# A hybrid decoder layer on one core: the ends of two feed-forwards, one place in the mixer and the start are put in another order

## The chip, the cores and the metric

The kernel runs on one core of one Trainium2 chip. A core has five engines that run beside each other, each with its own instruction stream: TensorE (PE) multiplies matrices into PSUM, VectorE (DVE) and ScalarE (ACT) work on elements, GpSimd (POOL) does small things here, and SyncE (SP) issues most transfers. The metric is the device time of one execution in microseconds (us).

## The reference, cut to what matters

One decoder layer over 512 tokens of width 1024:

```
h = x + 1/2 * SwiGLU_1(RMSNorm(x))                # 1024 -> 2816 -> 1024
z = RMSNorm(h) @ W_in                             # q, k, v | gla q, k, v, gate rank, out gate
A = sliding_window_attention(q, k, v, sinks)      # 8 heads of 64, window 128
B = RMSNorm(gated_linear_attention(...)) * silu(gate)
h = h + concat(A, B) @ W_out
h = h + 1/2 * SwiGLU_2(RMSNorm(h))
h = h + sigmoid(RMSNorm(h) @ W_g) * RMSNorm(p @ W_p)
```

All of it is in float32.

## The kernel before, in words

The 512 tokens are four tiles of 128 (`h[0]` to `h[3]`). Every large product is three matmuls (`mm3`): both operands are split into a high part in fp32r and the rest, also fp32r, and hi·hi, hi·lo and lo·hi are added in PSUM. Weights come as "units" of 1 MB or 512 KB (`W`): a transfer that SP issues into `wraw`, a cast on ScalarE to `whi`, a subtraction on VectorE to `wlo` (`split`, L140 and L141; in the first two units every second subtraction is GpSimd's). `W.get` splits the unit that is asked for and some ahead; a third number says how far ahead.

A norm of one tile has five steps: two squares with a running sum on ScalarE (`norm_squares`), the mean on VectorE and the power on GpSimd (`norm_factor`), the scaling on VectorE (`norm_scaled`), eight 128x128 transposes on TensorE into two PSUM banks and, for each bank, a cast `nhi` on ScalarE and a subtraction `nlo` on VectorE (`norm_transpose`). The gain of a norm lies in SBUF spread over 128 partitions; `gain_tile` gets it by a broadcasting transfer of 512 KB.

The stages follow each other: feed-forward 1 (`pg`, `pu`, `pd`), the mixer (`pe`, an embedding product; `kvr`, `aq`, `gqk`, `gv`, `gog`, the input projections; attention and the gated linear attention), the output projection `wo`, feed-forward 2, and the gate `pgt`. A scheduler writes the engines' streams in the order of the code, except where `on_pe` and `in_order` tie a step behind the last instruction of TensorE, or of TensorE, ScalarE and VectorE. So these lists of steps are the order: `last_tiles` for the end of a feed-forward (last down products of a tile, the update of `h`, its norm), and the long list that ends with `gla_mix` for the mixer. An engine's stream runs in order: what waits holds what is behind it.

Four places matter here.

- The start. SP asks for the first tile of x, the spread gain of the first norm, the second tile, the first two weight units and the other two tiles. The first product covers tiles 0 and 1 (columns 0 to 256), once with the gate's weights and once with the up weights.
- The end of feed-forward 1. `pe` of tiles 0 and 1 stands on TensorE behind the transposes of tiles 0 and 1 (`ntr_mx`), and its bank is one that the last update of `h[3]` has to read out first.
- The mixer. `turn_decay` transposes decayed keys in three pieces `kdt0` to `kdt2`, one after the other, into a pool of two banks (`psG`), and ScalarE copies each to `kdT`. Later four `gla_out` steps give `o0` to `o3`, and `gla_mix` their transposes `otr`.
- The end of feed-forward 2. The units of the gate's weights (`wraw135` and on) are split between the norms; `split_gates` asks for the first. Then `pgt` runs over two halves of the columns and four tiles; the last one is done in two parts of 256 columns.

Of the kernel before, what the change touches and what calls it, by code (L numbers as in the profile page):

```python
# [152 lines left out]
def hymba_kernel(tc, A, out):  # L153
# [457 lines left out]
    for t in range(0, NT, 2):  # L611
        eo = mp.tile([P, 8, 256], F32, name=f"eo{t}", tag="e", bufs=2).rearrange("p (t a) c -> p t (a c)", t=2)
        for i in range(2):
# [5 lines left out]
            if t + i in (1, 2):  # L619
                turned[0](t + i + 1)  # L620
# [377 lines left out]
    with tc.tile_pool(name="ffn2p", bufs=1, reuse_waits="tile") as fp:  # L998
# [39 lines left out]
        def split_gates():  # L1038
            W.get(("pg", 0, 0), 0)
# [88 lines left out]
```

## Time and profile before

| | us |
|---|---|
| median of 3 runs | 1008.62 (1008.01 to 1010.85) |
| the profiled execution | 1008.22 |
| span of its instructions | 1006.5 |
| TensorE busy | 971.2 |
| VectorE busy | 645.0 |
| ScalarE busy | 394.5 |

The profile is of one execution. Its span runs from the first to the last instruction, and 1.7 us lie around it. TensorE is busy for 96% of the span; what it waited for is listed by line in a view of its own. The profile also gives for each stretch the clock that was granted to TensorE, as a share of the full one (1.00 is 2.4 GHz, 0.50 is 1.2 GHz). Busy TensorE at 0.50 counts as busy.

### The profile page before, as it was taken

How to read it: one execution, taken by the hardware profiler on the slowest of the kernel's cores; microseconds unless marked ns; L12 is line 12 of the kernel's file. 1: busy time of each engine (PE TensorE's matmuls, PEld its weight loads, DVE VectorE, ACT ScalarE, POOL GpSimd, SP SyncE). 2: the span in 40 equal slices, each digit the busy share in tenths (PEclk: the TensorE clock that was granted, in tenths of full speed). 3: DMA queues.
4: the chain of work that ended last, by engine and by line, in shares of the span. 5: the costliest groups of instructions: out<-in, count | busy, mean ns of one | idle time of the engine just before them, and what ended most of it. 6: DMA issues, size and time to landing. Idle time of an engine off the chain costs nothing.

```text
span 1006.5 us, 12373 instructions
## 1 busy us (share of the span) xinstructions
PE 971.2 (96%) x5090; PEld 807.4 (80%) x5090; DVE 645.0 (64%) x811; ACT 394.5 (39%) x569; POOL 43.7 (4%) x55
## 2 busy tenths in 40 slices
PE   5999999999999989998998999999999999999898
PEld 5988888888888879876766789888888888888687
DVE  6567667576675764775766364766677675757652
ACT  5443333333333245585455243333344333332441
POOL 4000000000000010200002010000000000000010
PEclk9999999999999999999998999999999999999999
DMA  8715133141330255220213246142252523303231
GB/s 290 250 47 168 41 126 125 46 167 40 126 105 1 88 186 184 88 85 1 58 50 98 84 163 242 42 168 84 96 205 75 169 83 106 124 1 104 74 126 53
DMA packets 74235, 109.91 MB, mean 109 GB/s; under 512 B 5937, under 2 KB 55234, under 8 KB 74178
## 3 DMA queue, kind: packets, MB, share of 16 engines
q1 hardware_dynamic: 72450, 102.82, 30.4%
q0 software_dynamic: 1728, 6.29, 1.8%
q8 instruction: 40, 0.66, 0.2%
q14 instruction: 17, 0.14, 0.0%
HBM read 100.72 MB, written 8.39 MB: 108 GB/s over the span
## 4 chain that ended last, share of the span: by engine, by line
PE 88%; DVE 6%; ACT 2%; DMA 2%; issue 1%; POOL 0%; SPq 0%; ACTq 0%; POOLq 0%; DVEq 0%
PE pg L199 24%; PE pu L199 24%; PE pd L199 20%; PE pgt L199 5%; PE wo L199 4%; PE aq L199 2%; PE pe L199 1%; PE kvr L199 1%; PE gqk L199 1%; PE gv L199 1%; PE gog L199 1%; DVE mx L724 1%; DMA wraw<-in_w_out_dram 1%; DVE wlo L141 1%; DVE e L722 1%
## 5 line engine op out<-in xcount | busy, mean ns | idle before, releaser
L140 ACT CAST whi<-wraw 128x1024 fp32r<-128x1024 f32 (+1 forms) x126 | 129.9, 1039 | 187.4 <-PE pd L199 136.3
L141 DVE TENSOR_TENSOR wlo<-wraw,whi 128x1024 fp32r<-128x1024 f32 (+1 forms) x124 | 149.9, 1215 | 56.0 <-ACT whi L140 53.7
L199 PE MATMUL pg<-nlo_f,whi 128*128 128x512 f32 (+1 forms) x384 | 143.0, 373 | 0.0
L199 PE MATMUL pg<-nhi_f,whi 128*128 128x512 f32 (+1 forms) x384 | 142.6, 373 | 0.2 <-ACT nhi_f L292 0.2
L199 PE MATMUL pu<-nhi_f,wlo 128*128 128x512 f32 (+1 forms) x384 | 142.6, 372 | 0.0
L199 PE MATMUL pg<-nhi_f,wlo 128*128 128x512 f32 (+1 forms) x384 | 142.6, 372 | 0.0
L199 PE MATMUL pu<-nlo_f,whi 128*128 128x512 f32 (+1 forms) x384 | 142.6, 372 | 0.0
L199 PE MATMUL pu<-nhi_f,whi 128*128 128x512 f32 (+1 forms) x384 | 142.4, 372 | 0.0
L199 PE MATMUL pd<-whi,ahi 128*128 128x512 f32 x312 | 121.4, 389 | 0.0
L199 PE MATMUL pd<-wlo,ahi 128*128 128x512 f32 x312 | 121.4, 389 | 0.0
L199 PE MATMUL pd<-whi,alo 128*128 128x512 f32 x312 | 120.6, 389 | 0.0
L391 DVE SCALAR_TENSOR_TENSOR h<-pd,h 128x512 f32<-128x512 f32 x116 | 76.5, 686 | 29.5 <-PE pd L199 29.5
L199 PEld LDWEIGHTS pg<-nhi_f,whi 128*128 128x128 f32 x384 | 72.3, 189 | 13.2 <-ACT nhi_f L292 0.7
L199 PEld LDWEIGHTS pg<-nlo_f,whi 128*128 128x128 f32 x384 | 72.6, 189 | 12.9 <-DVE nlo_f L293 0.6
L199 PEld LDWEIGHTS pg<-nhi_f,wlo 128*128 128x128 f32 x384 | 72.5, 189 | 12.5
L199 PEld LDWEIGHTS pu<-nhi_f,wlo 128*128 128x128 f32 x384 | 72.3, 188 | 12.5
L199 PEld LDWEIGHTS pu<-nhi_f,whi 128*128 128x128 f32 x384 | 72.2, 188 | 12.5
L199 PEld LDWEIGHTS pu<-nlo_f,whi 128*128 128x128 f32 x384 | 72.4, 188 | 12.3
L140 ACT CAST whi<-draw 128x1024 fp32r<-128x1024 f32 x35 | 36.8, 1053 | 96.9 <-PE pu L199 50.9
L431 DVE TENSOR_TENSOR cb<-pu,sg 128x512 f32<-128x512 f32 x44 | 30.3, 690 | 69.2 <-PE pu L199 69.2
L140 ACT CAST whi<-wpr 128x1024 fp32r<-128x1024 f32 x35 | 36.9, 1053 | 96.2 <-PE pu L199 58.2
L199 PEld LDWEIGHTS pd<-whi,ahi 128*128 128x128 f32 x312 | 58.6, 188 | 12.2
(243 smaller groups left out, 1466.5 us busy)
## 6 DMA issues: line engine op xcount, KB each, us to landing
wraw<-in_ffn_w_gate_dram SPq DMA_DIRECT2D x22, 1024.0 KB, 5.0
wraw<-in_ffn_w_up_dram SPq DMA_DIRECT2D x22, 1024.0 KB, 5.0
wpr<-in_ffn_w_down_dram SPq DMA_DIRECT2D x10, 1024.0 KB, 5.6
draw<-in_ffn_w_down_dram SPq DMA_DIRECT2D x10, 1024.0 KB, 5.2
wraw<-in_w_in_dram SPq DMA_DIRECT2D x8, 1024.0 KB, 4.9
wraw<-in_ple_w_gate_dram SPq DMA_DIRECT2D x4, 1024.0 KB, 4.8
h<-in_x_dram SPq DMA_DIRECT2D x4, 512.0 KB, 7.0
wraw<-in_ffn_w_down_dram SPq DMA_DIRECT2D x4, 512.0 KB, 3.4
```

The lines of the kernel that those rows point to most:

```text
L140: nc.scalar.copy(hi, v)
L141: (nc.gpsimd if u < 2 and i else nc.vector).tensor_tensor(lo, v, hi.bitcast(F32), op=ALU.subtract)
L199: last_pe[0] = nc.tensor.matmul(o, lhsT=l, rhs=r, start=start, stop=stop_, **kw).ins
L391: nc.vector.scalar_tensor_tensor(hs, x, 0.5, hs, ALU.mult, ALU.add)
L431: nc.vector.tensor_mul(cb[:, half].rearrange("p a c -> p (a c)"), pu, sg)
L722: nc.vector.tensor_add(half, sc[:, :, :, :nk], amask[:, 256 - nk:].unsqueeze(1).unsqueeze(1).broadcast_to([P, 2, 2, nk]))
L724: nc.vector.reduce_max(mxt.rearrange("p (g a) -> p g a", g=2)[:, :, 2 * a:2 * a + 2], half, AX.X)
```

## The change

The edits are at the four places: the ends of both feed-forwards, the mixer, and the start.

```diff
+    def gain_by_pe(name):
+        row, ones = w4(f"row_{name}")[0:1, :], w4(f"ones_{name}")[0:1, :P]
+        nc.sync.dma_start(out=row, in_=A[name].rearrange("(one d) -> one d", one=1))
+        nc.vector.memset(ones, 1.0)
+        t = w4(f"gain_{name}")
+        for c in range(2):
+            ps = psT(f"gain_{name}{c}")
+            mm(ps, ones, row[:, c * 512:c * 512 + 512], True, True)
+            nc.scalar.copy(t[:, c * 512:c * 512 + 512], ps)
         return t
...
-        for k0 in (0, 4):
-            W.add_rows("pg", A["ple_w_gate"], k0, 4, c0, 512)
+        for k0, nk in ((0, 2), (2, 2), (4, 4)) if c0 == 0 else ((0, 4), (4, 4)):
+            W.add_rows("pg", A["ple_w_gate"], k0, nk, c0, 512)
...
-        in_order((pd, 0, 0), (pd, 1, 0), (pd, 0, 1), (update, 0), (squares, 0), (pd, 1, 1), (update, 1), (factor, 0),
-                 (squares, 1), (pd, 2, 0), (pd, 2, 1), *third, (scaled, 0), (update, 2), (factor, 1), (squares, 2),
-                 (pd, 3, 0), (pd, 3, 1), (scaled, 1), *fourth, (turned, 0), (update, 3), (factor, 2), (squares, 3),
-                 (scaled, 2), (turned, 1), (factor, 3), (scaled, 3))
+        in_order((pd, 0, 0), (pd, 1, 0), (pd, 0, 1), (update, 0), (squares, 0), (pd, 1, 1), (update, 1), (squares, 1),
+                 (factor, 0), (pd, 2, 0), (pd, 2, 1), (scaled, 0), (factor, 1), (update, 2), (scaled, 1),
+                 (pd, 3, 0), (pd, 3, 1), *((named.get(f, f), *args) for f, *args in places))
...
-                gemm(1, 0, 256)
+                on_pe(gemm, 1, 0, 256)
...
+    g1 = gain_by_pe("ffn1_norm")
     nc.sync.dma_start(out=h[0], in_=A["x"][0:P, :])
-    g1 = gain_tile("ffn1_norm", nc.sync)
...
-            turned.append(last_tiles(pd, update, lambda: gm, nTm, "mx", (), [(keep, 0), (keep, 1), (keep, 2)]))
-            keep(3)
+            turned.append(last_tiles(pd, update, lambda: gm, nTm, "mx", [
+                ("update", 3), ("turned", 0), ("squares", 2), ("factor", 2), ("turned", 1), ("squares", 3),
+                (keep, 0), (keep, 1), ("scaled", 2), ("factor", 3), (keep, 2), (lambda: W.get(("kvr", 0, 0), 0),),
+                ("scaled", 3), (keep, 3)]))
...
-            if t + i in (1, 2):
-                turned[0](t + i + 1)
+            if t + i < 2:
+                turned[0](t + i + 2)
...
-    def turn_decay():
-        kdC = Xs.pop("k")
-        for c in range(3):
-            ...
-            nc.scalar.copy(kdT[:, c], ps[:, :256].rearrange("p (a c) -> p a c", a=2))
+    def turn_decay(c):
+        kdC = Xs["k"]
+        ...
+        nc.vector.tensor_copy(kdT[:, c], ps[:, :256].rearrange("p (a c) -> p a c", a=2))
...
-            (weighted, 3), (gla_gate, 3, 0), (gla_out, 0), (gla_silu, 0), (gla_out, 1), (gla_silu, 1),
-            (gla_gate, 3, 1), (gla_silu, 2), (gla_silu, 3), (attention_out,), (gla_out, 2),
-            (gla_mix, 0, mixT), (gla_out, 3), (gla_mix, 1, mixT), (out_half, 0, 0), (out_half, 0, 1),
+            (weighted, 3), (gla_gate, 3, 0), (gla_out, 0), (gla_out, 1), (gla_gate, 3, 1), (gla_out, 2),
+            (gla_silu, 0), (gla_silu, 1), (attention_out,), (gla_out, 3), (gla_silu, 2), (gla_silu, 3),
+            (gla_mix, 0, mixT), (gla_mix, 1, mixT), (out_half, 0, 0), (out_half, 0, 1),
...
-            turned[:] = [last_tiles(pd, update, lambda: g3[0], nT3, "pg", [(split_gates,)])]
+            split_gates(0)
+            turned[:] = [last_tiles(pd, update, lambda: g3[0], nT3, "pg", [
+                ("squares", 2), ("turned", 0), ("factor", 2), (split_gates, 2), (split_gates, 4), ("turned", 1),
+                ("scaled", 2), ("update", 3), ("squares", 3), ("factor", 3), ("scaled", 3)])]
...
-                if c0 == 0 and t in (1, 2):
-                    turned[0](t + 1)
-                parts = ((0, 256), (256, 512)) if c0 and t == NT - 1 else ((0, 512),)
+                parts = ((0, 384), (384, 512)) if c0 and t == NT - 1 else ((0, 512),)
...
+                    if c0 == 0:
+                        on_pe(gemm_ts, ps, nT3, t, wt[:2], False)
+                        if t in (1, 2):
+                            on_pe(turned[0], t + 1)
+                        on_pe(gemm_ts, ps, nT3, t, wt[2:], True, 4)
+                    else:
+                        gemm_ts(ps, nT3, t, wt)
```

In the mixer's list the three `turn_decay` steps stand apart now: `turn_decay 0` behind `gla_diagonal` (`gd`), `turn_decay 1` before `gla_state 0`, `turn_decay 2` behind `weighted 1`.

ScalarE's stream at the start, from the second tile's squares to the third's, before:

```order
L307 ACTIVATE nrm_f11_134,ss_f11_135<-h1_92 128x512 x2
L292 CAST nhi_f1_99<-ntr_f10_0_120 128x4x128
L292 CAST nhi_f1_99<-ntr_f10_1_127 128x4x128
L140 CAST whi0_0_255<-wraw0_105 128x1024
L140 CAST whi0_1_259<-wraw0_105 128x1024
L292 CAST nhi_f1_99<-ntr_f11_0_143 128x4x128
L140 CAST whi1_0_263<-wraw1_107 128x1024
L140 CAST whi1_1_267<-wraw1_107 128x1024
L292 CAST nhi_f1_99<-ntr_f11_1_150 128x4x128
L307 ACTIVATE nrm_f12_157,ss_f12_158<-h2_93 128x512 x2
```

and now (`nrm_f1t` are the squares of tile t, `nhi_f1<-ntr_f1t` its high parts, `whi0` and `whi1` the casts of the first two weight units):

```order
L319 ACTIVATE nrm_f11_143,ss_f11_144<-h1_92 128x512 x2
L140 CAST whi0_0_264<-wraw0_114 128x1024
L140 CAST whi0_1_268<-wraw0_114 128x1024
L304 CAST nhi_f1_99<-ntr_f10_0_129 128x4x128
L304 CAST nhi_f1_99<-ntr_f10_1_136 128x4x128
L140 CAST whi1_0_272<-wraw1_116 128x1024
L140 CAST whi1_1_276<-wraw1_116 128x1024
L319 ACTIVATE nrm_f12_166,ss_f12_167<-h2_93 128x512 x2
L304 CAST nhi_f1_99<-ntr_f11_0_152 128x4x128
L304 CAST nhi_f1_99<-ntr_f11_1_159 128x4x128
```

The casts of the first unit stand ahead of tile 0's high parts, and tile 1's high parts stand behind the second unit's casts and behind the third tile's squares.

VectorE's stream at the end of the first feed-forward, from tile 2's update on, before (`h3` is the update of tile 3, `wlo62` the low parts of the first `kvr` weights):

```order
L391 SCALAR_TENSOR_TENSOR h2_93<-pd1_0_2_2606,h2_93 128x512
L391 SCALAR_TENSOR_TENSOR h2_93<-pd1_1_2_2610,h2_93 128x512
L312 SCALAR_TENSOR_TENSOR ms_mx1_2623<-ss_mx1_2603 128x1
L316 SCALAR_TENSOR_TENSOR nrm_mx1_2602<-h1_92,rs_mx1_2625,gain_mix_norm_239 128x1024
L141 TENSOR_TENSOR wlo62_0_2804<-wraw62_2800,whi62_0_2803 128x544
L141 TENSOR_TENSOR wlo62_1_2808<-wraw62_2800,whi62_1_2807 128x544
L293 TENSOR_TENSOR nlo_mix_242<-ntr_mx0_0_2649,nhi_mix_241 128x4x128
L293 TENSOR_TENSOR nlo_mix_242<-ntr_mx0_1_2656,nhi_mix_241 128x4x128
L391 SCALAR_TENSOR_TENSOR h3_94<-pd1_0_3_2631,h3_94 128x512
L391 SCALAR_TENSOR_TENSOR h3_94<-pd1_1_3_2635,h3_94 128x512
L312 SCALAR_TENSOR_TENSOR ms_mx2_2665<-ss_mx2_2628 128x1
L316 SCALAR_TENSOR_TENSOR nrm_mx2_2627<-h2_93,rs_mx2_2667,gain_mix_norm_239 128x1024
```

and now:

```order
L403 SCALAR_TENSOR_TENSOR h2_93<-pd1_0_2_2615,h2_93 128x512
L403 SCALAR_TENSOR_TENSOR h2_93<-pd1_1_2_2619,h2_93 128x512
L328 SCALAR_TENSOR_TENSOR nrm_mx1_2607<-h1_92,rs_mx1_2632,gain_mix_norm_248 128x1024
L403 SCALAR_TENSOR_TENSOR h3_94<-pd1_0_3_2637,h3_94 128x512
L403 SCALAR_TENSOR_TENSOR h3_94<-pd1_1_3_2641,h3_94 128x512
L305 TENSOR_TENSOR nlo_mix_251<-ntr_mx0_0_2653,nhi_mix_250 128x4x128
L305 TENSOR_TENSOR nlo_mix_251<-ntr_mx0_1_2660,nhi_mix_250 128x4x128
L324 SCALAR_TENSOR_TENSOR ms_mx2_2671<-ss_mx2_2668 128x1
L305 TENSOR_TENSOR nlo_mix_251<-ntr_mx1_0_2675,nhi_mix_250 128x4x128
L305 TENSOR_TENSOR nlo_mix_251<-ntr_mx1_1_2682,nhi_mix_250 128x4x128
L328 SCALAR_TENSOR_TENSOR nrm_mx2_2667<-h2_93,rs_mx2_2673,gain_mix_norm_248 128x1024
L324 SCALAR_TENSOR_TENSOR ms_mx3_2696<-ss_mx3_2690 128x1
```

The update of tile 3 stands ahead of the low parts of tile 0 now, and `wlo62`, which stood between them, comes after the scaling of tile 2.

TensorE's stream in the mixer, behind the first values `gv_0`, before:

```order
L199 MATMUL pv0_3571<-pb0_0_3445,vr_2799 64x512 x2
L202 MATMUL kdt0_3575<-idn_81,kd_3476 128x128 x2
L202 MATMUL kdt1_3579<-idn_81,kd_3476 128x128 x2
L202 MATMUL kdt2_3583<-idn_81,kd_3476 128x128 x2
L199 MATMUL gd_3587<-gqT_2992,gkT_2993 64x64 x32
L202 MATMUL pt1_0_3621<-idn_81,e1_3355 128x128 x8
L199 MATMUL gv_1_3638<-whi68_0_3006,nhi_mix_241 128x512
```

and now:

```order
L199 MATMUL pv0_3580<-pb0_0_3454,vr_2819 64x512 x2
L199 MATMUL gd_3584<-gqT_3001,gkT_3002 64x64 x32
L202 MATMUL kdt0_3618<-idn_81,kd_3485 128x128 x2
L202 MATMUL pt1_0_3622<-idn_81,e1_3364 128x128 x8
L199 MATMUL gv_1_3639<-whi68_0_3015,nhi_mix_250 128x512
```

Of the three `kdt` one is left here, behind `gd`; `kdt1` stands 27 rows further down, ahead of `dS0`, and `kdt2` another 30 rows down, behind `pv1`.

## Rows read from the trace of the kernel before

**Rows 1.** Heading of the page; busy time, share and instructions of each engine.
```profile
span 1006.5 us, 12373 instructions
PE 971.2 (96%) x5090; PEld 807.4 (80%) x5090; DVE 645.0 (64%) x811; ACT 394.5 (39%) x569; POOL 43.7 (4%) x55
```

**Rows 2.** What TensorE waited for: line waited for, total us, times, longest.
```profile
PE ntr_f L202 <- DVE nrm_f L316: 8.2, 1, 8.2
PE kdt L202 <- ACT kdT L893: 3.9, 1, 3.9
PE o L199 <- DVE on L932: 3.7, 2, 3.5
PE ntr_pg L202 <- ACT whi L140: 3.7, 1, 3.7
PE pe L199 <- DVE h L391: 2.5, 1, 2.5
PE pt L202 <- ACT pb L751: 2.4, 2, 2.0
PE ntr_pg L202 <- DVE nrm_pg L316: 1.0, 1, 1.0
```

**Rows 3.** Stretches: length, busy us (instructions) by engine, PEclk, DMA share, GB/s.
```profile
100.00:110.00 10.00, 10.00 (x46) 8.29 (x45) 6.73 (x8) 4.19 (x4) 0.00 (x0) 1.00 0.31 105
366.63:369.12 2.49, 0.00 (x1) 0.00 (x0) 2.49 (x6) 0.54 (x2) 0.00 (x0) 1.00 0.48 112
369.12:376.52 7.40, 7.38 (x26) 5.87 (x27) 3.86 (x6) 2.77 (x7) 3.08 (x6) 0.77 0.59 236
376.52:378.30 1.78, 1.78 (x17) 1.78 (x16) 0.21 (x1) 1.74 (x3) 0.00 (x0) 1.00 0.11 41
462.00:465.90 3.90, 0.08 (x1) 0.00 (x0) 0.21 (x2) 3.90 (x18) 0.00 (x0) 1.00 0.00 0
465.90:470.00 4.10, 4.07 (x75) 3.62 (x76) 2.94 (x5) 3.27 (x7) 0.00 (x0) 0.58 0.00 0
540.30:544.40 4.10, 0.65 (x4) 0.42 (x4) 3.80 (x8) 1.94 (x4) 1.32 (x1) 1.00 0.73 259
948.00:954.90 6.90, 2.29 (x17) 2.11 (x17) 6.90 (x10) 3.70 (x8) 1.40 (x1) 0.94 0.66 192
954.90:961.80 6.90, 6.90 (x28) 5.62 (x27) 5.73 (x9) 3.58 (x7) 2.94 (x4) 0.81 0.30 113
996.70:1002.40 5.70, 5.70 (x49) 5.61 (x47) 2.23 (x4) 0.98 (x2) 0.00 (x0) 1.00 0.18 69
```

**Rows 4.** DMA view of the first 20 us: GB/s in 40 slices.
```profile
GB/s 0 0 0 156 279 393 270 172 197 238 270 369 401 381 369 360 381 385 387 387 385 385 385 387 426 408 438 418 434 375 387 355 135 29 22 41 102 120 243 261
```

**Rows 5.** ScalarE at the start: start, us, instruction [idle before <- releaser].
```profile
10.74 1.99 ACT L140 CAST whi<-wraw 128x1024 fp32r<-128x1024 f32 x2
13.18 0.59 ACT L292 CAST nhi_f<-ntr_f 128x512 fp32r<-128x512 f32 x1 [0.45 <-PE ntr_f L202]
13.66 2.00 ACT L140 CAST whi<-wraw 128x1024 fp32r<-128x1024 f32 x2
16.04 0.64 ACT L307 ACTIVATE nrm_f<-h 128x512 f32<-128x512 f32 x1
```

**Rows 6.** TensorE at the start: first two matmuls of the feed-forward.
```profile
13.82 0.80 PE L199 MATMUL pg<-nhi_f,whi 128*128 128x256 f32 x2
```

**Rows 7.** VectorE at the first feed-forward's end.
```profile
365.34 1.35 DVE L141 TENSOR_TENSOR wlo<-wraw,whi 128x544 fp32r<-128x544 f32 x2
367.81 1.28 DVE L391 SCALAR_TENSOR_TENSOR h<-pd,h 128x512 f32<-128x512 f32 x2
```

**Rows 8.** ScalarE in the mixer: the first two key copies.
```profile
465.52 0.62 ACT L893 COPY kdT<-kdt 128x256 f32<-128x256 f32 x2
```

**Rows 9.** VectorE at the second feed-forward's end.
```profile
949.98 2.35 DVE L141 TENSOR_TENSOR wlo<-wraw,whi 128x1024 fp32r<-128x1024 f32 x2
```

**Rows 10.** ScalarE: a cast of activations near the second feed-forward's end.
```profile
932.35 0.62 ACT L433 CAST ahi<-cb 128x512 fp32r<-128x512 f32 x1 [11.19 <-DVE cb L431]
```

More of the change, by code (lines that the diff above doesn't have):

```diff
@@ L234, in gain_tile @@
         return t
+    def gain_by_pe(name):
[7 more added lines that the diff above has]
+            nc.scalar.copy(t[:, c * 512:c * 512 + 512], ps)
+        return t
     hpool = ExitStack()
@@ L322, in norm, with last_tiles @@
         return t, nrm, nT, name
-    def last_tiles(pd, update, gain, nT, name, third=(), fourth=()):
+    def last_tiles(pd, update, gain, nT, name, places):
         sq, rs = {}, {}
@@ L339, in turned @@
             norm_transpose(t, sq[t][0], nT, name, (psA, psG))
-        in_order((pd, 0, 0), (pd, 1, 0), (pd, 0, 1), (update, 0), (squares, 0), (pd, 1, 1), (update, 1), (factor, 0),
-                 (squares, 1), (pd, 2, 0), (pd, 2, 1), *third, (scaled, 0), (update, 2), (factor, 1), (squares, 2),
-                 (pd, 3, 0), (pd, 3, 1), (scaled, 1), *fourth, (turned, 0), (update, 3), (factor, 2), (squares, 3),
-                 (scaled, 2), (turned, 1), (factor, 3), (scaled, 3))
+        named = {"pd": pd, "update": update, "squares": squares, "factor": factor, "scaled": scaled, "turned": turned}
+        in_order((pd, 0, 0), (pd, 1, 0), (pd, 0, 1), (update, 0), (squares, 0), (pd, 1, 1), (update, 1), (squares, 1),
+                 (factor, 0), (pd, 2, 0), (pd, 2, 1), (scaled, 0), (factor, 1), (update, 2), (scaled, 1),
+                 (pd, 3, 0), (pd, 3, 1), *((named.get(f, f), *args) for f, *args in places))
         return turned
@@ L885, in gla_decay @@
         Xs["k"] = kdC
-    def turn_decay():
-        kdC = Xs.pop("k")
-        for c in range(3):
-            ps = psG(f"kdt{c}")
-            for a in range(2):
-                turn(ps[:, a * P:(a + 1) * P], kdC[:, a * 4 + c, :])
-            nc.scalar.copy(kdT[:, c], ps[:, :256].rearrange("p (a c) -> p a c", a=2))
+    def turn_decay(c):
+        kdC = Xs["k"]
+        ps = psG(f"kdt{c}")
+        for a in range(2):
+            turn(ps[:, a * P:(a + 1) * P], kdC[:, a * 4 + c, :])
+        nc.vector.tensor_copy(kdT[:, c], ps[:, :256].rearrange("p (a c) -> p a c", a=2))
     def gla_state(c):
@@ L975, in hymba_kernel @@
             (gla_qk, 3), (gla_decay,), (gla_decays, 0), (scores, 2),
-            (gla_v, 0), (weighted, 0), (turn_decay,), (gla_diagonal,), (turn_scores, 1, 0), (gla_decays, 1),
-            (gla_v, 1), (gla_level, 0), (gla_state, 0), (turn_scores, 1, 1), (gla_decays, 2),
-            (gla_v, 2), (gla_level, 1), (weighted, 1), (gla_state, 1), (scores, 3), (gla_decays, 3),
+            (gla_v, 0), (weighted, 0), (gla_diagonal,), (turn_decay, 0), (turn_scores, 1, 0), (gla_decays, 1),
+            (gla_v, 1), (gla_level, 0), (turn_decay, 1), (gla_state, 0), (turn_scores, 1, 1), (gla_decays, 2),
+            (gla_v, 2), (gla_level, 1), (weighted, 1), (turn_decay, 2), (scores, 3), (gla_state, 1), (gla_decays, 3),
             (gla_v, 3), (gla_level, 2), (gla_state, 2), (turn_scores, 2, 0), (gla_decays, 4),
@@ L1037, in hymba_kernel, with split_gates @@
         nT3 = norm_pair(np_, "pg")
-        def split_gates():
-            W.get(("pg", 0, 0), 0)
+        def split_gates(k):
+            W.get(("pg", 0, k), 0)
         def finish2(pd, update):
-            turned[:] = [last_tiles(pd, update, lambda: g3[0], nT3, "pg", [(split_gates,)])]
+            split_gates(0)
+            turned[:] = [last_tiles(pd, update, lambda: g3[0], nT3, "pg", [
+                ("squares", 2), ("turned", 0), ("factor", 2), (split_gates, 2), (split_gates, 4), ("turned", 1),
+                ("scaled", 2), ("update", 3), ("squares", 3), ("factor", 3), ("scaled", 3)])]
         ffn(2, nT2, fp, finish2, xp, xp, "nhi", 2, lambda: norm_transpose(*pend2[NT - 1]), embedding_norm)
@@ L1062, in hymba_kernel @@
                     ps = psA(f"pgt{c0}_{t}_{a}")[:, :b - a]
-                    gemm_ts(ps, nT3, t, [(wh[:, :, a:b], wl[:, :, a:b]) for wh, wl in tiles])
+                    wt = [(wh[:, :, a:b], wl[:, :, a:b]) for wh, wl in tiles]
+                    if c0 == 0:
[5 more added lines that the diff above has]
+                        gemm_ts(ps, nT3, t, wt)
                     sg = op.tile([P, 512], F32, name=f"sgm{c0}_{t}_{a}", tag="sgm", bufs=3)[:, :b - a]
```

## The prediction

> **What bounds the kernel now.** The page's head comes first: TensorE is busy for 971.2 of 1006.5 us [rows 1], so nothing but the remaining 35 us, the half-speed stretches inside the busy time and the two ends can move. The second view lists what TensorE waited for [rows 2]: 8.2 us before the first transposes, then six waits of 1.0 to 3.9 us. Four of these stand where the change moves steps: kdt 3.9, ntr_pg 3.7 and 1.0, pe 2.5. The third view is a table of stretches around those places [rows 3]. It shows a second cost that the list of waits hides: behind each of the three longer holes the granted clock of the next stretch is below one (0.77, 0.58, 0.81, against 1.00 in the stretches where TensorE never paused). The clock has two levels, 2.4 and 1.2 GHz, so 0.77 over 7.40 us means 0.23 x 7.40 = 1.7 us lost. Last come the instruction lists of ScalarE and VectorE at each place [rows 5, 7 to 10], to see what the releasing instruction stood behind.
>
> **The change part by part.** The sum is made against the profiled execution, 1008.2 us, which is 0.4 under the median.
>
> *The end of feed-forward 1.* `pe` waits 2.5 us for the update of tile 3. VectorE did the low parts of the kvr weights (1.35 us) and tile 0's low parts (1.28 us, the time from 366.61 to the update at 367.81 is 1.2) and only then, at 367.81, that update [rows 7]. Both now stand behind it, so it starts 1.35 + 1.2 = 2.55 us earlier, about 365.3, and ends at 366.5. TensorE comes free at 366.63 [rows 3]. The hole of 2.5 us goes, and with it the reason for the slow stretch behind: 1.7 us by the row above. What is late next is the transposes of tile 3, whose scaling now stands behind the kvr low parts; I put 0.4 us on it. The twelve kvr matmuls that move ahead of `pe` 2 are the same work. Together -2.5 - 1.7 + 0.4 = -3.8; the ends are -4.2 (no new wait) and -1.0 (half of the hole stays and is enough to slow the clock as before).
>
> *The mixer's keys.* `kdt2` found both banks of its pool taken, because the copy of `kdt0` stood in ScalarE's queue behind the exponentials: ScalarE was busy for 3.90 of 3.90 us (18 instructions) while TensorE did nothing [rows 3], and the copy started at 465.52 [rows 8]. Now the copies are VectorE's and one `kdt` at a time is followed by other matmuls, so nothing asks for a third bank. The wait of 3.9 goes, and 0.42 x 4.10 = 1.7 of the slow stretch behind it. Three copies of about 0.31 us each (two took 0.62 on ScalarE) go to VectorE, beside TensorE's gv matmuls, which cover them; without cover they cost 0.9. Sum -5.6, ends -6.0 and 0. The second is the first rival.
>
> The Trainium skill, page "TensorE: Matmul & The Clock Gate", section on architectural detail, states that ScalarE and VectorE take their queues in strict order; this wait, for a copy whose transposes were long done, agrees.
>
> *The mixer's end.* `o` waits 3.5 us for VectorE [rows 2], and in that hole TensorE did 0.65 us of transposes of the first output [rows 3]. These now stand behind `o3`, whose wait has not moved: its bank is freed by the same chain. They come after the hole, so +0.7; ends 0 and +1.1 (the same work at half the clock).
>
> *The end of feed-forward 2.* Transposes of tile 0 wait 1.0 and those of tile 1 3.7 us [rows 2]. VectorE did the low parts of two gate units (2.35 us) at 949.98, ahead of the scaling of tile 1 [rows 9]. Now the first unit is only half as big and split before the tiles' updates, and the other splits stand behind the transposes of tile 0, so both scalings are done before TensorE asks. -4.7 and 0.19 x 6.90 = 1.3 for the clock behind [rows 3]. Against it: `pgt` now needs the low parts of units 136 and 137 just in time, three of 1.18 us one after the other; I put 0.5 on it. Sum -5.5; ends -6.0 and -2.0 (three low parts in a row stand on the path: +3.5, and the clock gain stays).
>
> *The last tile.* Its two parts of 256 columns become 384 and 128. 256 columns cost 5.70/49 = 0.116 us each, 512 cost 10.00/46 = 0.217 [rows 3]; between them 384 cost 0.167, 24 of them 4.0. No row shows such a matmul with 128 columns. The line through the two gives 0.066 (1.6 for 24), 128-column transposes 1.78/17 = 0.105 (2.5), and the price of 512 columns as the upper end 5.2. I take the transposes, the nearest row. Before, 48 matmuls took 5.6; now 4.0 + 2.5 = 6.5. Sum +0.9, ends 0 and +3.6. The shorter last sigmoid, product and store I count at nothing.
>
> The same page of the Trainium skill gives, in its section "Back-to-back issue gap", 81 ns for a sustained matmul of 128 columns and 131 ns for one of 512. The second is not what the trace has (217 ns). By the first the 24 would take 1.9 and this term would be +0.3, an estimate from that page.
>
> *The start.* The gain's 512 KB no longer go through the queue; a row of 4 KB takes their place in the issues. At the 172 to 393 GB/s that the transfers ran at then [rows 4] this is 1.3 to 3.0 us; I take 1.5 for the arrival of the first weight unit, which was in at 10.74 at the latest, when its casts started [rows 5]: now 9.2. But ScalarE's stream has changed. Before, it did tile 1's first high part at 13.18, and 0.05 us after that cast's end the first product started, at 13.82 [rows 5, 6]. Now the order is the first unit's casts (2.0 us, to 11.2), tile 0's high parts (1.0, to 12.2), the second unit's casts (2.0, to 14.2; that unit was in by 13.66 before), the third tile's squares (two of 0.64, about 1.2 from start to start of the next, to 15.4), and only then tile 1's first high part (0.59, to 16.0). So the first product starts at 16.0 instead of 13.8. From there to the end of feed-forward 1 TensorE has no wait, so this shift stays: +2.2. The ends: +0.8 if the units come 3.0 us earlier and the second at 10.7, and +4.1 if the third tile comes no earlier than 16.04, when its squares ran before [rows 5]. The two matmuls that spread the gain and their copies lie in the 8.2 us in which TensorE had nothing to do. The second `gemm` tied behind the first changes only whose matmul comes first.
>
> Sum: -3.8 - 5.6 + 0.7 - 5.5 + 0.9 + 2.2 = -11.1. From 1008.2 that is 997.1, and 0.4 more against the median: 997.5 us.
>
> **The rivals.**
>
> The mixer's gain comes back as a later wait: 0.15. For it speaks that the mixer has further waits, 2.4 us of `pt` for `pb` [rows 2], and that what releases them hangs on transfers and on ScalarE, not on TensorE's pace; an earlier TensorE would only wait longer there. Against it, the issue of these transfers is itself bound to steps that move along. Then the 5.6 are lost: 1003.1. If in this case the narrow part and the start also come out at their upper ends (+2.7 and +1.9), nothing measurable is left, 1007.7; I give that 0.05 of the 0.15.
>
> The narrow matmul is dear: 0.14. 128 columns cost as much as 512 and the last tile +3.6 instead of +0.9: 1000.2. For it, no row has the shape and the pieces of a matmul that don't depend on columns are unknown; against it, the transposes.
>
> The start gets no later: 0.08. If tile 1's high parts did not in effect stand behind the third tile's squares, the earlier arrival would count in full, -1.5 instead of +2.2: 993.8. Against it stands the order of ScalarE's stream, and the copy that waited in it.
>
> Slower than before: 0.03. The cast of the first gate unit now stands in ScalarE's queue ahead of the last casts of activations, of which the first ran at 932.35 after 11.19 us of idleness [rows 10]. If that unit's data or its place in the ring came late, the activations would wait, and the last down products with them. It costs nothing up to about 931.3, and the whole gain is spent when the cast starts 11.1 us after that, at 942.4; at 945 the time would be 1011. Against it, the idle 11.19 us say that the weights ahead of it had come long before.
>
> **How the numbers follow.** The forecast has 0.60, the rivals 0.15, 0.14, 0.08 and 0.03. The forecast's own range is 994 to 1001, from the ends of its terms, which would not all fall on one side. The range down to the early start's 993.8 with a little of the terms' ends, 992.5, and up over the first rival, 1003.5, leaves out the worst of that rival, the slow case, and some on the low side. A difference of 0.3%, 3 us, is about what a measurement of this kernel can tell from none. Faster by more than that are the forecast, the narrow part, the early start and two thirds of the first rival: 0.92 with the ends cut off. Within 0.3%: 0.05. Slower: 0.03.
>
> **What would show it.** In the list of TensorE's waits the lines of kdt, ntr_pg and pe are gone or below 0.5 us. The stretches behind them have a granted clock of 1.00. The first `pg` starts near 16.0, with ScalarE's third squares directly ahead of tile 1's high part. The wait of `o` is still near 3.5 us, and longer if anything. The 24 matmuls of 128 columns take 2.5 us together. The prediction is wrong if the wait for `pb` grows by several us, if a new line above 2 us stands in the list behind feed-forward 1, or if the first product starts before 14.

## The result

The changed kernel takes 998.22 us (median of 4 runs, 998.0 to 998.88); the kernel before, run beside it on the same chip, 1008.32. The ratio is 0.99, with a 95% interval of 0.9876 to 0.9924: faster by 1.0%. The forecast was 997.5. But one of its terms was too small by 3 us, and other stages that came out better, one of them by chance, made up for most of that, so the sum says less than the stages do.

The head of the profile after, to be held against [rows 1]: TensorE is busy for the same 971 us, in a span that is 10.0 us shorter.

```profile
span 996.5 us, 12390 instructions
PE 971.3 (97%) x5094; PEld 806.5 (81%) x5094; DVE 646.3 (65%) x815; ACT 394.5 (40%) x568; POOL 42.6 (4%) x55
```

The list of what TensorE waited for [rows 2] has lost kdt 3.9, pe 2.5 and ntr_pg 3.7 and 1.0. What stands in it now (left out: the first transposes' wait of 2.4 for the scaling, the gain's row with 2.3, and a wait of `pt` of 1.4 that before has too; columns as there):

```profile
PE o L199 <- DVE on L945: 4.5, 2, 4.4
PE pt L202 <- ACT pb L765: 2.7, 2, 1.9
PE ntr_f L202 <- DVE nlo_f L305: 2.6, 1, 2.6
PE wo L199 <- DVE wlo L141: 1.7, 1, 1.7
PE pg L199 <- ACT nhi_f L304: 1.6, 2, 1.4
PE pg L199 <- DVE nlo_f L305: 1.1, 1, 1.1
PE ntr_mx L202 <- DVE nrm_mx L328: 0.4, 1, 0.4
PE pgt L199 <- DVE nlo_pg L305: 0.3, 1, 0.3
```

The waits of `pg` at the start are 2.7 us together, where before has 0.2. `ntr_mx` has the 0.4 that the prediction put on tile 3's transposes, and `pgt` 0.3. The wait of `o` is longer, 4.4 at most instead of 3.5. The stretches that answer to [rows 3], with the clock in the third column from the end: `pe`, the values behind the first keys, `o3`, the first two stretches of `pgt`, and the first product at the start:

```profile
371.37:377.07 5.70, 5.70 (x29) 4.70 (x28) 4.95 (x10) 4.55 (x13) 1.97 (x3) 1.00 0.22 92
464.59:470.33 5.74, 5.74 (x29) 4.48 (x29) 2.29 (x5) 5.09 (x17) 0.00 (x0) 1.00 0.01 3
539.00:542.80 3.80, 3.79 (x17) 2.90 (x17) 2.52 (x5) 0.00 (x0) 1.01 (x1) 0.50 0.01 2
944.53:949.00 4.47, 4.38 (x18) 3.28 (x19) 4.39 (x6) 4.45 (x6) 1.57 (x1) 1.00 0.29 71
949.00:953.40 4.40, 4.40 (x22) 3.60 (x21) 4.26 (x6) 3.00 (x6) 0.00 (x0) 1.00 1.04 404
18.25:22.00 3.75, 3.75 (x17) 3.75 (x18) 3.29 (x10) 0.00 (x0) 1.79 (x2) 1.00 1.04 302
```

The first two and the two of `pgt` stand at 1.00 where before had 0.77, 0.58 and 0.81. `o3` runs at 0.50 as before. The last row is odd, and the start below comes back to it: 17 matmuls in 3.75 us, at a clock that reads 1.00.

Where the 10 us went can be read stage by stage from TensorE's instruction lists: the time from one mark to the next, in us, for the profiled execution of each kernel. The marks are the end of the last down product of feed-forward 1, the first `gqk`, the first `gog`, the first `o`, the first `wo`, the last `wo`, the last down product of feed-forward 2, and the last matmul's end.

| kernel | to end of `pd` 1 | to `gqk` | to `gog` | to `o` | to `wo` | `wo` | to end of `pd` 2 | to the last matmul |
|---|---|---|---|---|---|---|---|---|
| before | 364.63 | 57.40 | 75.02 | 34.79 | 17.15 | 49.70 | 349.22 | 54.61 |
| after | 369.87 | 53.68 | 69.27 | 33.54 | 18.00 | 49.12 | 349.21 | 49.87 |
| difference | +5.24 | -3.72 | -5.75 | -1.25 | +0.85 | -0.58 | 0.0 | -4.74 |

From the last matmul to the execution's end it is 5.7 us in both. The differences add up to -9.95; the profiled times differ by 10.0.

One profile does not fix a stage to the tenth. Over the kernels below, the first stage takes 364.63 to 365.46 us with the old start and 368.85 to 369.87 with the new one. The stage to `o` is 1.6 to 2.7 us longer in three of the profiles (before, parts_256, best): there the granted clock fell to 0.50 for 3.4 us behind the first wait of `pt` for `pb`, in the others it did not.

### The profile page after: what moved, and what is told of

Read it like the earlier page. It is cut to its first block, busy times and chain, and to the rows that moved or that the text cites. A ratio compares the mean times of both kernels' runs of the same rounds, so it can differ in the third digit from the quotient of the medians.

```text
span 996.5 us, 12390 instructions
## 1 busy us (share of the span) xinstructions
PE 971.3 (97%) x5094; PEld 806.5 (81%) x5094; DVE 646.3 (65%) x815; ACT 394.5 (40%) x568; POOL 42.6 (4%) x55
## 4 chain that ended last, share of the span: by engine, by line
PE 88%; DVE 6%; ACT 2%; DMA 2%; issue 1%; POOL 0%; SPq 0%; ACTq 0%; DVEq 0%; POOLq 0%
PE pg L199 24%; PE pu L199 24%; PE pd L199 21%; PE wo L199 4%; PE pgt L199 3%; PE aq L199 2%; PE gv L199 2%; PE kvr L199 1%; PE gqk L199 1%; DMA wraw<-in_ffn_w_gate_dram 1%; DVE wlo L141 1%; DMA wraw<-in_w_out_dram 1%; ACT whi L140 1%; DMA emb<-emb_d 1%; DVE e L736 1%
## 5 line engine op out<-in xcount | busy, mean ns | idle before, releaser
L199 PEld LDWEIGHTS pd<-whi,alo 128*128 128x128 f32 x312 | 58.6, 188 | 12.2
```

The costliest lines, as they stand in the source:

```text
L199: last_pe[0] = nc.tensor.matmul(o, lhsT=l, rhs=r, start=start, stop=stop_, **kw).ins
```

## The experiments

All twelve ran in three groups, each beside new runs of the kernel before, whose medians were 1006.78 (start_ kernels without start_warm), 1007.07 (keys_undone, outs_undone, parts_256, start_warm) and 1006.86 (the rest). The kernel before itself spreads from 1004.4 to 1008.8 in them. So a part is sized by its own stage in the trace, and the medians only confirm it.

**start_undone** takes back the start alone:

```diff
-    g1 = gain_by_pe("ffn1_norm")
     nc.sync.dma_start(out=h[0], in_=A["x"][0:P, :])
+    g1 = gain_tile("ffn1_norm", nc.sync)
...
-                on_pe(gemm, 1, 0, 256)
+                gemm(1, 0, 256)
```

> The changed kernel with the start of before (spread gain by transfer, second gemm not tied). Counted from the two traces, the first product's later start (2.55 us), the wait behind it (1.1) and a longer slow stretch (about 1.6) make the start cost 5.2 us, and everything behind it is independent of it. By that theory 993.0 us. Rival: only the later first product (2.2 to 2.6) is the start's, the rest is lost elsewhere before 40 us whatever the start: 995.8.

993.53 us, 0.9873 of before (0.986 to 0.9886). Feed-forward 1's down products end at 365.20 instead of 369.87, 4.7 us earlier; the stages up to the first `o` differ by less than 0.05. The start costs 4.7 of the 5.2 expected, and the 995.8 of the rival is out.

**start_alone** is the kernel before with only the new start (the same lines the other way).

> The kernel before with only the new start. If the start costs 5.2 us by itself: 1008.3 + 5.2 = 1013.5, slower. Rival, the cost is only the 2.2 us of the prediction: 1010.5. A second rival, that before has room for it in the waits behind (feed-forward 1's end waits on engines that would not be late): 1008 to 1009.

1010.44 us, 1.0033 of before (1.002 to 1.0046): the only kernel here that is slower. Its first stage ends at 368.85, 4.2 us after before's, but the whole is only 3.7 longer; to `gqk` it needs 56.78 instead of 57.40, since `pe` waits 1.9 instead of 2.5. Two more stages differ, both with the length of a stretch at the lower clock: to `gog` it is 76.29 instead of 75.02 (6.8 us at 0.50 behind the keys' wait, before has 3.4), and to `o` 32.83 instead of 34.79 (none behind the wait for `pb`, before has 3.4). The time is that of the first rival, 1010.5, but beside a before of 1006.78 and not 1008.3. The direction is that of the first theory, the size lies between it and the prediction's, and part of it is the first weights' transfer: their casts start at 8.98 here and at 9.76 in the profile of after.

What the start consists of, in after. First ScalarE, with the columns of [rows 5]:

```profile
9.76 1.99 ACT L140 CAST whi<-wraw 128x1024 fp32r<-128x1024 f32 x2 [1.85 <-DMA wraw<-in_ffn_w_gate_dram]
11.65 1.06 ACT L304 CAST nhi_f<-ntr_f 128x512 fp32r<-128x512 f32 x2
12.61 2.00 ACT L140 CAST whi<-wraw 128x1024 fp32r<-128x1024 f32 x2
14.50 0.64 ACT L319 ACTIVATE nrm_f<-h 128x512 f32<-128x512 f32 x1
...
15.74 1.06 ACT L304 CAST nhi_f<-ntr_f 128x512 fp32r<-128x512 f32 x2
```

The order is the one foreseen: casts, tile 0's high parts, casts, tile 2's squares, then tile 1's high parts at 15.74. The first unit's casts began at 9.76 and not at 9.2. Then VectorE and, in a fence of its own, GpSimd:

```profile
15.87 1.72 DVE L324 SCALAR_TENSOR_TENSOR ms_f<-ss_f 128x1 f32<-128x1 f32 x1 [0.50 <-ACT nrm_f L319]
17.52 0.68 DVE L305 TENSOR_TENSOR nlo_f<-ntr_f,nhi_f 128x512 fp32r<-128x512 f32 x1
```

```profile
14.69 2.89 POOL L141 TENSOR_TENSOR wlo<-wraw,whi 128x1024 fp32r<-128x1024 f32 x1 [0.40 <-ACT whi L140]
```

The mean of tile 2, an operation of one column, took 1.72 us and ended at 17.59. GpSimd's low part of the second unit ended at 17.58. Tile 1's low part stood behind it on VectorE. And TensorE:

```profile
8.49 1.97 PE L202 MATMUL ntr_f<-idn,nrm_f 128*128 128x128 f32 x8 [2.43 <-DVE nrm_f L328]
...
16.37 0.80 PE L199 MATMUL pg<-nhi_f,whi 128*128 128x256 f32 x2 [1.38 <-ACT nhi_f L304]
18.25 0.58 PE L199 MATMUL pg<-nlo_f,whi 128*128 128x256 f32 x1 [1.09 <-DVE nlo_f L305]
18.63 0.42 PE L199 MATMUL pg<-nhi_f,wlo 128*128 128x256 f32 x1
18.85 0.42 PE L199 MATMUL pg<-nhi_f,whi 128*128 128x256 f32 x1
...
23.30 0.28 PE L199 MATMUL pg<-nhi_f,whi 128*128 128x256 f32 x1
23.41 0.28 PE L199 MATMUL pg<-nlo_f,whi 128*128 128x256 f32 x1
```

The first product starts at 16.37 (before 13.82), its third matmul at 18.25 (before 14.55), and then its matmuls are 0.214 us apart until 23.30 and 0.12 after that. Before, the spacing was 0.12 from 15.51 on. So the loss is 2.55 for the later high part, 1.1 for the wait on the low part, and about 18 more matmuls x 0.095 = 1.7 for the slow spacing: 5.3.

The slow spacing is the lower clock. The trace's first clock record, at the full clock, begins at 23.24 in after and at 15.41 in before, which is where the spacing changes; the column counts time without a record as 1.00 and so doesn't show it. The transposes agree: the eight at 8.49 took 1.97 us, and in end2_undone below eight take 1.94 at a granted 0.50 and 1.06 at 1.00. With the old start the first record begins between 15.41 and 17.50 (before, start_undone, best), with the new one between 21.61 and 23.69 (after, start_alone and six kernels below that keep it).

**start_turned** ties tiles 2 and 3 of the first norm behind tile 1's high parts:

```diff
-    for t in range(NT):
-        norm_transpose(*norm(t, g1, nT1, "f1"))
+    for t in range(2):
+        last = norm_transpose(*norm(t, g1, nT1, "f1"))
+    with tc.issue_after(last):
+        for t in range(2, NT):
+            norm_transpose(*norm(t, g1, nT1, "f1"))
```

> The changed kernel with one tie more: tiles 2 and 3 of the first norm are behind tile 1's high parts, so ScalarE does tile 1's high parts right after the second unit's casts (at 14.5 instead of 15.74), and VectorE does tile 1's low parts ahead of tile 2's mean, the tiny operation that took 1.72 us. Theory, the order on these two engines is the cause: first product at 15.1, no wait between first and third matmul beyond 0.7, so 2.5 to 4.5 us faster: 994 to 995.7. Rival, the cause is the new order on TensorE (all pg before pu) or the transfers: 998.

994.79 us. The first stage ends at 366.34, 3.5 us before after's. The two waits of `pg` are down from 2.7 to 0.7 us, the first product starts at 14.38. TensorE's order, pg before pu, is as in after, so that is not the cause; what stands ahead of tile 1's parts on ScalarE and VectorE is. The first unit also came earlier here than in after (casts from 8.99 on); against parts_256, whose casts start at 8.96 and whose first stage takes 369.07, the tie is worth 2.7.

**start_best** also puts the first unit's casts between the high parts of tiles 0 and 1 and the second unit's behind them:

```diff
+    n0, n1 = norm(0, g1, nT1, "f1"), norm(1, g1, nT1, "f1")
+    last = norm_transpose(*n0)
+    with tc.issue_after(last):
+        W.get(("g1", 0), 0)
+    last = norm_transpose(*n1)
+    with tc.issue_after(last):
+        W.get(("u1", 0), 0)
+        for t in range(2, NT):
+            norm_transpose(*norm(t, g1, nT1, "f1"))
```

> The changed kernel with the start tied in this order on ScalarE: squares 0 and 1, tile 0's high parts, first unit's casts, tile 1's high parts, second unit's casts, squares 2 and 3. Theory, the order on ScalarE and VectorE is the cause: first product at about 13.7 us, like before: 992 to 993.5. Rival, transfers or TensorE's own order: 998.

993.23 us, 0.9874 of before (0.9859 to 0.9888), level with start_undone. TensorE at the start:

```profile
13.55 0.80 PE L199 MATMUL pg<-nhi_f,whi 128*128 128x256 f32 x2 [0.43 <-ACT nhi_f L304]
14.28 0.58 PE L199 MATMUL pg<-nlo_f,whi 128*128 128x256 f32 x1
```

The first product is 0.3 us earlier than before's, but its matmuls are 0.214 apart up to 18.0 (the first clock record begins at 17.99), longer than before's. The first stage ends at 365.36, 0.7 us after before's: the slow stretch takes back what the saved transfer gives at the first product.

**start_warm** adds twelve matmuls of the identity with itself to start_best, seven ahead of the gain's and five behind:

```diff
+    warm_ps = psA("warm")
+    for _ in range(7):
+        mm(warm_ps[:, :P], idn, idn, True, True)
     g1 = gain_by_pe("ffn1_norm")
+    with tc.issue_after(last_pe[0]):
+        for _ in range(5):
+            mm(warm_ps[:, :P], idn, idn, True, True)
```

> The kernel start_best with twelve matmuls of the identity with itself (their result is used by nothing) on TensorE in its first idle 8 us: seven before the gain is spread, five after. In start_best the first product's matmuls are 0.214 us apart for 4.5 us and 0.118 from 18.0 us on, though the stretch's clock column says 1.00. Theory, this is the clock at its lower level after the idle start: with TensorE at work earlier the spacing is 0.118 from the first product or soon after, 1.5 to 2.2 us faster than start_best: 991 to 991.7. Rival, the spacing comes from the operands still being written (VectorE and GpSimd at work beside it): 993.2, or up to 0.5 more from the added matmuls.

997.29 us, 4 us over start_best's median; in the profiles it is 3.0, all of it in the first stage (368.53 against 365.36). A miss. TensorE:

```profile
1.35 3.35 PE L199 MATMUL warm<-idn 128*128 128x128 f32 x14 [1.35 <-POOL idn masks.py:199]
4.64 3.78 PE L199 MATMUL gain_ffn_norm<-row_ffn_norm,ones_ffn_norm 1*128 1x512 f32 x4
8.35 2.50 PE L199 MATMUL warm<-idn 128*128 128x128 f32 x10
...
16.59 0.58 PE L199 MATMUL pg<-nlo_f,whi 128*128 128x256 f32 x1
...
20.39 0.38 PE L199 MATMUL pg<-nhi_f,wlo 128*128 128x256 f32 x1
20.60 0.28 PE L199 MATMUL pg<-nhi_f,whi 128*128 128x256 f32 x1
```

The added matmuls took more time than the expectation allowed for (3.35 us for the first seven, which are two instructions each in the list), held back the gain's matmuls from 2.3 to 4.64 and so the whole start by 2.3 us. And the slow spacing stayed: from 16.59 to 20.6, behind a TensorE that had been at work since 1.35 with only short pauses. Of the theory one half holds: 0.214 is what 256 columns take at 1.2 GHz, and the first clock record, at the full clock, begins at 20.59, where the spacing changes. The other half, that an earlier beginning shortens it, falls in this form. What makes the clock rise when it does stays open.

**keys_undone** puts the three key transposes and their copies back as before (ScalarE copies, `turn_decay` in one piece ahead of `gla_diagonal`).

> The changed kernel with the mixer's keys as before: three transposes in a row, copies on ScalarE. Theory (the copy behind the exponentials held TensorE for 3.9 us and the slow stretch behind cost 1.7): the wait of kdt is back near 3.9 and the time is 5.6 us longer, 1003.8; if the slow stretch at the next pt wait comes back as well (it went with the change, 1.6 us by the traces), 1005.4. Rival, the wait is mostly hidden by later waits on transfers: 998.5 to 1000.

1003.02 us, 0.9965 of before (0.9952 to 0.9978). To `gog` it needs 75.05 us, within 0.05 of before's 75.02, so the part is worth 5.8 there. The wait of kdt is back:

```profile
PE kdt L202 <- ACT kdT L907: 3.9, 1, 3.9
PE pt L202 <- ACT pb L765: 1.9, 2, 1.6
```

The two waits of `pt` for `pb` are 0.8 below after's 2.7, and to `o` it is 32.78 against 33.54: a seventh of the gain comes back as these waits, as the first rival had it, and no more. This is not chance: where the clock stayed at 1.00 in that stage it takes 32.73 to 32.83 in the three kernels with the three transposes in a row (start_alone, keys_undone, keys_dve) and 33.49 to 33.77 in the eight that spread them.

**keys_dve** leaves the three transposes in a row too, but keeps the copies on VectorE; and at the start it gives GpSimd's part of the second unit to VectorE:

```diff
-            nc.scalar.copy(kdT[:, c], ps[:, :256].rearrange("p (a c) -> p a c", a=2))
+            nc.vector.tensor_copy(kdT[:, c], ps[:, :256].rearrange("p (a c) -> p a c", a=2))
...
-                (nc.gpsimd if u < 2 and i else nc.vector).tensor_tensor(...)
+                (nc.gpsimd if u < 1 and i else nc.vector).tensor_tensor(...)
```

The first hunk stands against before's lines.

> Two edits at places far apart, read from the trace each. (1) The mixer's key transposes stand in a row as before, but their copies are on VectorE as in the changed kernel. Theory, the queue of ScalarE alone made the wait: the wait of kdt is below 0.7 us and the first key-value product of the next tile comes no later than in the changed kernel, within 0.5 us. Rival, the order is needed: a wait of 2 us or more is back, and 3 to 5 us with it. (2) At the start the second unit's second low part is VectorE's instead of GpSimd's. Theory, the mean of tile 2 took 1.72 us because GpSimd's long operation ran until it ended: now it takes 0.16, and the wait of pg for tile 1's low part shrinks from 1.1 to 0.6. Rival, it is slow for another reason (its operand comes late): it stays near 1.7. Time if both theories hold: 997 to 998.

997.54 us. The wait for a key copy is gone, and the copies run on VectorE at once; the one wait left, 0.3, is for a bank that another copy on ScalarE frees:

```profile
PE kdt L202 <- ACT araw L777: 0.3, 1, 0.3
```

```profile
462.43 0.42 DVE L907 COPY kdT<-kdt 128x256 f32<-128x256 f32 x1
463.19 0.76 DVE L907 COPY kdT<-kdt 128x256 f32<-128x256 f32 x2 [0.33 <-PE kdt L202]
```

The first product of the next state (`dS`) comes 0.75 us later than in after, counted from the first `gqk`, which is beyond the 0.5 expected; to `gog` it needs 69.50, 0.23 more than after; and to `o` 32.73, 0.8 less. So the engine that copies makes the whole gain. Spreading the three transposes gains 0.2 us and loses 0.8 behind it, in the waits for `pb` (1.9 here, 2.7 in after). At the start, VectorE:

```profile
16.71 0.15 DVE L324 SCALAR_TENSOR_TENSOR ms_f<-ss_f 128x1 f32<-128x1 f32 x1
16.78 0.68 DVE L305 TENSOR_TENSOR nlo_f<-ntr_f,nhi_f 128x512 fp32r<-128x512 f32 x1
```

With no GpSimd operation beside it the mean of tile 2 takes 0.15 us instead of 1.72. That the long one had waited for GpSimd is shown by this. The Trainium skill, page "Trainium Architecture — The Big Picture", section "What this means for kernel authors", says that VectorE and GpSimd share a pair of ports under an exclusive lock; the two ends at 17.58 and 17.59 agree. The wait of `pg` for tile 1's low part shrinks from 1.1 to 0.1 us, more than expected, but the first stage with 369.41 stays among those of the kernels with the same start: here the weights came late (casts from 10.04 on), and the first clock record begins at 23.07, about as late as in after.

**outs_undone** gives the mixer's end its old order (`gla_mix 0` ahead of `gla_out 3`, and the `gla_silu` steps where they were).

> The changed kernel with the mixer's end as before (first output's transposes ahead of the fourth output). Theory, these transposes filled a hole that is still there: 0.7 to 0.9 us faster, 997.4. Rival, the place doesn't matter, since the output projection waits for the weights' low parts anyway: 998.2.

997.37 us. To `wo` it needs 17.13, 0.87 less, as expected. But the first `wo` product then takes 6.83 instead of 6.24 us, and the whole of `wo` 49.69 instead of 49.12. The row of that first product in outs_undone, and then the one of after:

```profile
543.25:550.08 6.83, 6.83 (x28) 5.54 (x27) 2.91 (x5) 0.59 (x1) 3.12 (x5) 0.83 0.53 176
```

```profile
544.36:550.60 6.24, 6.24 (x28) 5.11 (x27) 2.69 (x5) 0.71 (x2) 3.11 (x5) 0.91 0.61 195
```

With the old order more of the slow clock behind the hole falls on `wo`. The slow stretch itself does not move: it is 538.80 to 545.63 here, and in after

```profile
538.65:545.48 6.83, 6.47 (x27) 5.41 (x28) 4.53 (x10) 1.77 (x3) 1.96 (x2) 0.50 0.00 1
```

but `wo` comes 1.1 us earlier. Both stages together: 66.82 against 67.12. The ten kernels with the new order need 66.32 to 67.59 for the two, the four with the old one 66.78 to 66.87. So the change's cost here, if there is one, is lost in that spread; it is not 0.7 to 0.9.

**parts_256** gives the last tile its two parts of 256 columns back.

> The changed kernel with the last tile in two parts of 256 columns as before. The trace has 24 matmuls of 384 columns in 4.19 us and 24 of 128 in 2.66, and two times 24 of 256 took 5.75; from TensorE's last matmul to the end it is 3.9 us in both. So 1.0 us faster: 997.2. Rival, the shorter last store and sigmoid of 128 columns give the 1.0 us back: 998.2.

996.99 us. From the end of `pd` 2 to the last matmul it needs 48.51, in seven of the kernels with 384 and 128 it is 49.55 to 49.66 (49.87 in after, 50.13 in start_undone): 1.0 us less at the least. But from the last matmul to the end of the span it needs 4.37 us, against 3.88 to 3.90 in the kernels with 384 and 128 and the new end of feed-forward 2 (with the old end it is 3.94 in before and 3.45 in end2_undone). So half of the 1.0 comes back, as the rival had it: the last sigmoid and the product and the sum behind it are 0.4 us shorter with 128 columns. The last tile costs about 0.5 us in all, and the medians, 996.99 and 998.22 from different groups (ratios 0.9905 and 0.99), can't show it. The rows of the narrow parts, in after:

```profile
985.58 0.33 PE L199 MATMUL pgt<-whi,nhi_pg 128*128 128x384 f32 x1
...
989.77 0.22 PE L199 MATMUL pgt<-whi,nhi_pg 128*128 128x128 f32 x1
```

24 matmuls of 384 columns take 4.19 us and 24 of 128 2.66, 0.111 each: hardly less than 256 columns with 0.12.

**end1_undone** gives the end of feed-forward 1 its old order.

> The changed kernel with the end of feed-forward 1 as before. Theory, the update of tile 3 behind the kvr weights' low parts holds TensorE for 2.5 us and the slow stretch behind it costs 1.7: the wait of pe is back at 1.9 to 2.5 and the time is 3.7 us longer, 1001.9. Rival, a later wait (pt for pb, which hangs on a transfer) shrinks by as much: 999 to 1000.

1000.51 us, 0.9935 of before (0.9923 to 0.9947). To `gqk` it needs 56.79, 3.1 more than after. The wait of `pe` is back, shorter than before's 2.5, and behind it 3.4 us at the lower clock (374.48 to 377.89); 1.9 + 1.7 less the 0.4 of `ntr_mx` is 3.2:

```profile
373.41 0.50 PE L199 MATMUL pe<-whi,pTwhi 128*128 128x512 f32 x1 [1.91 <-DVE h L426]
```

**end2_undone** does the same for feed-forward 2, with the last tile's parts left at 384 and 128.

> The changed kernel with the end of feed-forward 2 as before (order of the splits and norms, one split unit of 1 MB, gate matmuls not halved; the last tile's parts stay 384 and 128). Theory, the low parts of two gate units ahead of the scaling of tile 1 cost 4.7 us of waits and 1.3 of slow clock: 5.9 us longer, 1004.1. Rival, only the longer wait of 3.7 is due to the order: 1002.

1003.38 us, 0.9965 of before (0.9952 to 0.9977). To the last matmul it needs 57.40, 7.5 more than after, where 5.9 was expected; before needed 54.6 and, with the dearer last tile added, would have needed 55.7. The waits of the transposes are 0.5 longer than before's, and TensorE works 5.9 us at 0.50 around the second (the clock is low from 947.53 to 954.35), before 3.4; half of the 2.5 more is 1.25. Together that is the 1.7 by which 57.40 lies above 55.7:

```profile
943.18 1.06 PE L202 MATMUL ntr_pg<-idn,nrm_pg 128*128 128x128 f32 x8 [1.04 <-DVE nrm_pg L328]
948.45 1.94 PE L202 MATMUL ntr_pg<-idn,nrm_pg 128*128 128x128 f32 x8 [4.20 <-DVE nrm_pg L328]
```

**best** takes back the start, the outputs' order and the last tile's parts, and keeps the two ends and the keys.

> The changed kernel with three of its edits taken back: the start, the outputs before the first transposes, and the parts of 384 and 128. If the three are independent: 998.2 - 4.7 - 0.85 - 1.2 = 991.5. Rival, an earlier TensorE waits longer for the weights of the output projection, whose place no edit moves: 992.5 to 993.5.

993.62 us, 0.9864 of before (0.9849 to 0.9879); not 991.5. It is level with start_undone. Two stretches of it, the gate product behind the wait for `pb` and the first `wo`, and the same two in start_undone:

```profile
498.32:505.66 7.34, 7.34 (x31) 5.62 (x32) 7.25 (x11) 3.29 (x8) 0.00 (x0) 0.77 0.01 2
540.50:547.48 6.98, 6.98 (x28) 5.62 (x27) 2.91 (x5) 0.59 (x1) 3.12 (x5) 0.81 0.48 168
```

```profile
497.63:503.35 5.72, 5.72 (x31) 4.48 (x33) 5.63 (x9) 2.38 (x6) 0.00 (x0) 1.00 0.01 3
539.32:545.05 5.73, 5.73 (x29) 4.69 (x28) 2.86 (x6) 0.91 (x2) 3.12 (x5) 1.00 0.52 192
```

In best both ran partly at the lower clock, 1.6 and 1.25 us more. The two stages of the outputs and `wo` need 66.87 in best and 66.32 in start_undone. The last stage gave 1.7, of which 0.5 goes back behind the last matmul. The wait for `pb` that stands ahead of the first stretch is 2.3 here and 1.9 there. The expected rival had the right time, but not by its wait: `wo` waits 1.7 for its weights' low parts here as in every kernel. What cost it was the clock behind the wait for `pb`. The earlier TensorE is not needed for that: parts_256, with the late start, has it too, behind a wait of 3.4,

```profile
503.22:506.64 3.42, 3.42 (x10) 2.64 (x9) 3.42 (x6) 0.44 (x1) 0.00 (x0) 0.50 0.02 5
```

and start_undone, start_turned and start_best, with an early TensorE, don't have it. Why the wait is longer in these executions stays open. The outputs' order, too, gave 0.25 here (66.87 against after's 67.12) where 0.85 was expected.

## Why the prediction was right, point by point

- *End of feed-forward 1*, predicted -3.8: measured -3.72. The 0.4 on tile 3's transposes is the wait of `ntr_mx`, 0.4. Taken back, it costs 3.1.
- *The keys*, -5.6: measured -5.75 up to `gog`, and 5.8 taken back. The reason was right (the copy behind the exponentials), but only one of the two edits was needed for it: copying on VectorE. The other, spreading the transposes, costs 0.7 to 0.8 in the waits behind, so the first rival came true in a small part; the two edits together are worth 5.0. The -1.25 that the table has up to `o` is these +0.7 and about -2.0 of luck: before's gate product ran at the lower clock there for 3.4 us (the stage takes 32.83 without that, in start_alone), after's did not.
- *The mixer's end*, +0.7: +0.85 up to `wo`, but about 0.6 comes back in `wo`. The step that took the transposes as filling a hole for nothing left out that the slow stretch behind the hole stays where it is, so that what TensorE has done earlier leaves more of the next product in it.
- *End of feed-forward 2 and the last tile*, -5.5 + 0.9 = -4.6: measured -4.74 up to the last matmul. The 2.35 us of [rows 9] are the two halves of one unit and not two units, which changes no sum. The last tile costs 1.1 up to the last matmul and so the end is worth 5.8. Behind it the shorter last sigmoid, product and store, which the prediction counted at nothing, give 0.5 back, and with the new end 0.4 more goes by there (4.37 against 3.94 us with two parts of 256): the two cancel. The price of 128 columns was taken at 0.105 from the transposes, and it is 0.111. The rival with the price of 512 columns is out.
- *The start*, +2.2: measured +5.24 in the profile, 4.7 when it is taken back and 4.2 in start_alone. This is the step that was mis-sized, beyond its upper end of 4.1. The chain on ScalarE came out as drawn (16.37 instead of 16.0, and 15.54 to 16.64 in the kernels with the same start). Missed were VectorE's queue, where a tiny operation ahead of tile 1's low part waits for GpSimd (1.1), and that TensorE is at the lower clock at the start and stays there longer with the new one (1.7).
- The slower rival (the gate unit's cast holding ScalarE at feed-forward 2's end) did not happen: the stage to the end of `pd` 2 is 349.2 in every kernel.

The sum came out at -9.95 against -11.1, since the start was 3.0 dearer, and the mixer's stages behind the keys together 1.7 cheaper than forecast. The 1.25 up to `o` among these 1.7 come of luck.

## What to carry to other kernels

A long wait of TensorE costs the hole and can cost half of a stretch at the lower clock with it. In the fourteen traces every wait of 2.5 us and more behind the start has such a stretch, none of 1.7 us and less has one, and of those between 1.9 and 2.3 some have. Where the order can take such a wait away, both are gained, and the place of a copy (which engine's queue) can matter more than the place of the work. When x or a weight comes earlier, look at what the engines' queues do with it: at the start ScalarE's new order cost 2.55 us, VectorE's wait for GpSimd 1.1 and the lower clock 1.7 more, and a saved transfer became a loss of 4 to 5 us. Undo the parts one by one: here the start lost more than the end of feed-forward 1 gained. And look at a stage in several executions before explaining a difference of one or two us in it.

## What the hardware showed that was not expected

- An operation of one column on VectorE (128x1) took 1.72 us, up to the end of GpSimd's operation of 128x1024, and 0.15 without that. In start_best one of 128x8 took 2.36 us, until 18.93, and GpSimd's ended at 18.89.
- 128 columns of fp32r cost 0.111 us, 256 0.12, 384 0.174 and 512 0.227: from 256 down, narrower saves nearly nothing.
- TensorE is at the lower clock at the start (eight transposes took 1.97 us at 8.49 in after, as 1.94 at a granted 0.50 in end2_undone). The first product's matmuls stand 0.214 us apart until 15.5 in before, 16.8 in start_undone, 18.0 in start_best, 20.6 in start_warm and 23.3 in after, where the trace's first clock record begins; the clock column reads 1.00 over all of it. TensorE's work since 1.35 us in start_warm did not end it.
- Where the slow stretch falls differs from execution to execution. At the same wait of `o`, 4.35 us, it begins 2.1 us before the wait's end in start_undone and 0.4 before it in after, 6.8 us long in both; in keys_dve it is 10.2 us long.
